# Where the next layer's conditioning sits in VectorE's queue during an MLP

## The chip, the cores and the metric

The kernel runs on one core of one Trainium2 chip. The metric is the device time of one execution in microseconds (us), as the median of several runs. The engines are named as in the profile: PE is TensorE's matmuls and PEld its weight loads, DVE is VectorE, ACT is ScalarE, POOL is GpSimd, and SP is SyncE, whose queue issues the loads that this text speaks of.

## The reference, cut to what matters

A transformer with 512 latent tokens, 256 context tokens and a width of 1024 runs two layers and then a second block with a mixture of experts. Every layer is conditioned on a vector: `silu(c) @ W + b` gives six vectors of 1024 (shift, scale and gate, for the mixer and for the MLP).

```python
def adaln(cond, w, b):
    return jnp.split(jax.nn.silu(cond) @ w + b, 6, axis=-1)

def squared_relu_mlp(h, w1, w2):
    return jnp.square(jax.nn.relu(h @ w1)) @ w2

# in each layer, after its mixer:
x = x + gt_m * squared_relu_mlp(modulate(x, sh_m, sc_m), mlp_w1[layer], mlp_w2[layer])
```

The MLP's hidden width is 4096. In layer 0 it also runs for the context tokens (768 tokens in all), in layer 1 for the 512 latent tokens alone. The conditioning of the latent tokens (`c`) needs all six vectors; that of the context (`c_ctx`) is computed for the first two.

## The kernel before

Activations lie transposed: eight tiles `x` of 128 features by 768 tokens. A product of full precision is made of three fast ones: weight and activation are each split into a high part (`wh`, `hh`) and a rest (`wl`, `hl`), and `dense` (L493) multiplies high by high, high by rest, rest by high. `load_w` brings a weight tile of 512 KB by SP's queue into one of three buffers, ACT makes `wh`, POOL makes `wl` (L471, L472, two buffers of each).

`mlp` works in four groups `g`. A group has eight **up tiles** (one weight tile each; PE fills a wide PSUM tile, of which there are two; ACT takes the ReLU into `u`, L615; DVE squares `u`, L616; ACT makes `hh`; DVE makes `hl`, L472) and then eight **down tiles** (one weight tile each; PE multiplies with the eight `hh` and `hl` of the group; DVE adds the result times the gate to `x`, L584, in `residual`). The first two up tiles are made together, as a pair. So each layer has 64 tiles: 32 up and 32 down. The first down tile of a group needs the `hh` and `hl` of the eighth up tile for the last eighth of its products.

Beside this, the MLP of one layer computes the conditioning of the next: `ada_side`. It needs 48 weight tiles `wside` of 128 x 1024 (512 KB each, two buffers, loaded by SP's queue, L457). A **pass** is one DVE instruction over such a tile (L460): multiply with the conditioning vector and sum along the row. The first two of the six vectors take two passes a tile, one for `c` and one for `c_ctx`; the others take one. That is 64 passes a layer. After the eighth tile of a vector a short instruction adds the bias (L462). The passes' list `side` is popped once per up tile and once per down tile, at the end of the tile's code:

```python
self.split(u[:, lo:hi], h[:, lo:hi], l[:, lo:hi])
hid.append((h, l))
if side:
    side.pop(0)()
```

The order of the code isn't the order in the engines' queues. The framework's scheduler orders each engine's instructions at build time, by which of them has its inputs ready in its own model of time; each engine then runs its queue strictly as written.

Of the kernel before, what the change touches and what calls it, by code (L numbers as in the profile page):

```python
# [10 lines left out]
F32 = mybir.dt.float32  # L11
# [4 lines left out]
ALU = mybir.AluOpType  # L16
# [6 lines left out]
D = 1024  # L23
# [282 lines left out]
class Kern:  # L306
# [135 lines left out]
    def ada_side(self, layer, pool):  # L442


        nc = self.nc
        cb = pool.tile([128, 2, D], F32, name="condb", bufs=1)
        nc.sync.dma_start(cb, self.i["cond"][layer - 1])
        nc.scalar.activation(cb, cb, AF.Silu)
        bias = self.p("ada_b_20" if layer == 2 else f"ada_b{layer}")

        def step(j, f):
            n = 2 if j < 2 else 1
            if f == 0:
                self.ada[layer, j] = self.const.tile([128, 8, 2], F32, name=f"ada{layer}_{j}")
            out = self.ada[layer, j]
            w = pool.tile([128, D], F32, tag="wside", name=self.uid("wside"), bufs=2)
            nc.sync.dma_start(w, self.i[f"ada{layer}"][8 * j + f])  # L457
            for q in range(n):
                o = pool.tile([128, D], F32, tag="side", name=self.uid("side"), bufs=1)
                nc.vector.scalar_tensor_tensor(o, w, 1.0, cb[:, q, :], op0=ALU.mult, op1=ALU.mult, accum_out=out[:, f, q:q + 1])  # L460
            if f == 7:
                nc.vector.scalar_tensor_tensor(out[:, :, :n], out[:, :, :n], 1.0 if j in (1, 4) else 0.0,  # L462
                                               bias[:, 8 * j:8 * j + 8, None].to_broadcast([128, 8, n]),
                                               op0=ALU.add, op1=ALU.add)

        return [lambda j=j, f=f: step(j, f) for j in (1, 0, 2, 4, 3, 5) for f in range(8)]


    def split(self, src, hi, lo, eng=None):
        nc = self.nc  # L470
        nc.scalar.activation(hi, src, AF.Copy)  # L471
        (eng or nc.vector).tensor_tensor(lo, src, hi.bitcast(F32), op=ALU.subtract)  # L472

    def load_w(self, src, n):

# [105 lines left out]

    def residual(self, x, ps, gt, f, parts):
        for q, (a, b) in enumerate(parts):
            self.nc.vector.scalar_tensor_tensor(x[:, a:b], ps[:, a:b], gt[:, f, q:q + 1], x[:, a:b],  # L584
                                                op0=ALU.mult, op1=ALU.add)


    def mlp(self, layer, parts):
        nc, tc = self.nc, self.tc
        lo, hi = parts[0][0], parts[-1][1]  # L590
        sh, sc, gt = (self.ada[layer, j] for j in (3, 4, 5))
        with tc.tile_pool(name=f"mlp{layer}", bufs=2, reuse_waits="tile") as pool:
            side = self.ada_side(layer + 1, pool)
            self.tb = 5

            def tmp(name):
                return pool.tile([128, TT], F32, tag="tmp", name=self.uid(name), bufs=self.tb)

            act = self.modulate(self.x, sh, sc, parts, pool)
            w1, w2 = self.i[f"mlp1_{layer}"], self.i[f"mlp2_{layer}"]  # L600

            first = self.dense_pair("up", [w1[0], w1[1]], act, parts)

            def up(g):
                hid = []
                for f in range(8 * g, 8 * g + 8):
                    if first:
                        ps = first.pop(0)
                    else:
                        ps = self.wide("up")  # L610
                        self.dense(ps, self.load_w(w1[f], 1024), act, parts)
                    u = pool.tile([128, TT], F32, tag="tmp", name=self.uid("u"), bufs=self.tb)
                    h = pool.tile([128, TT], F32R, tag="hh", name=self.uid("hh"), bufs=10)
                    l = pool.tile([128, TT], F32R, tag="hl", name=self.uid("hl"), bufs=10)
                    nc.scalar.activation(u[:, lo:hi], ps[:, lo:hi], AF.Relu)  # L615
                    nc.vector.tensor_tensor(u[:, lo:hi], u[:, lo:hi], u[:, lo:hi], op=ALU.mult)  # L616
                    self.split(u[:, lo:hi], h[:, lo:hi], l[:, lo:hi])
                    hid.append((h, l))
                    if side:
                        side.pop(0)()  # L620
                return hid

            if layer == 1:
                for k in range(KD):
                    nc.sync.dma_start(self.x[k][:, T:], self.i["ctx2T"][k])
            for g in range(4):
                hid = up(g)
                if g == 3:
                    acc = tmp("acc")
                for f in range(KD):  # L630
                    w = self.load_w(w2[g, f], 1024)
                    ps = self.wide("dn")
                    self.dense(ps, w, hid, parts)
                    self.residual(self.x[f], ps, gt, f, parts)
                    if g == 3:
                        self.squares_add(acc, self.x[f], f, PARTS, tmp, nc.gpsimd)
                    if side:
                        side.pop(0)()
            self.y = self.rstd_tokens(acc, PARTS)
            self.tb = 6  # L640

# [1815 lines left out]
```

## Time and profile before

| what | value |
|---|---|
| median of 3 runs | 3518.22 us (3511.94 to 3525.28) |
| the profiled execution's own time | 3523.28 us |
| span of that execution in the profile | 3521.4 us |
| MLP of layer 0 in the span | from about 588 to 1147 us |
| MLP of layer 1 in the span | from about 2221 to 2610 us |

The span runs from the first to the last instruction. A "wait" in the profile is the time that an engine stood idle before an instruction, with what ended it. An idle engine costs time only where something that sets the end waits for it.

### The profile page before, as it was taken

What the parts mean: (1) busy time and instruction counts of PE and PEld (TensorE: products, weight loads), DVE (VectorE), ACT (ScalarE), POOL (GpSimd) and SP (SyncE); (2) the same over time, 40 slices, a digit from 0 to 9 for tenths busy, and PEclk for the clock granted to TensorE, in tenths of its full rate; (3) what the DMA queues carried; (4) which work ended last, traced back from release to release, by engine and by line L of the source; (5) the groups of instructions that cost most, each with busy time, mean ns of one, the idle gap of its engine ahead of it and who ended that gap; (6) DMA issues with size and microseconds to landing.
All of it is one profiled execution on the core that took longest, in us unless ns stands there. A gap on an engine that the chain in (4) does not pass through costs nothing. (4 is left out here: it accounts for less than half of the span.)

```text
span 3521.4 us, 56690 instructions
## 1 busy us (share of the span) xinstructions
PE 3171.4 (90%) x23582; PEld 2413.3 (69%) x23582; DVE 1820.7 (52%) x3073; ACT 1320.0 (37%) x2503; POOL 913.9 (26%) x467
## 2 busy tenths in 40 slices
PE   7989998899999789589999998799999899799887
PEld 4666887788888677377887876677778677333333
DVE  5476664862322975477777763864342654222213
ACT  3232453211222543377777774322233453100001
POOL 1111113222324423422223212344443324100000
PEclk9999999999999899699999998999999999899999
DMA  5222222552222233200000103473332228799997
GB/s 220 96 72 84 84 73 96 186 185 66 64 63 98 85 106 109 69 18 28 28 28 28 31 8 114 161 251 126 94 115 67 75 78 274 274 420 421 420 421 312
DMA packets 126321, 488.44 MB, mean 139 GB/s; under 512 B 13360, under 2 KB 23024, under 8 KB 101744
## 3 DMA queue, kind: packets, MB, share of 16 engines
q1 hardware_dynamic: 119936, 477.40, 37.9%
q8 instruction: 186, 3.05, 0.4%
q0 software_dynamic: 1184, 4.20, 0.3%
q10 hardware_dynamic: 4944, 3.21, 0.3%
q14 instruction: 71, 0.58, 0.1%
HBM read 455.92 MB, written 28.84 MB: 138 GB/s over the span
## 5 line engine op out<-in xcount | busy, mean ns | idle before, releaser
L472 POOL TENSOR_TENSOR wl<-w,wh 128x1024 fp32r<-128x1024 f32 (+1 forms) x259 | 626.4, 2420 | 1602.2 <-ACT wh L471 1458.0
L471 ACT ACTIVATE wh<-w 128x1024 fp32r<-128x1024 f32 (+1 forms) x259 | 266.8, 1032 | 909.5 <-PE dn L493 333.6
L493 PE MATMUL dn<-hh,wh 128*128 128x512 f32 (+1 forms) x768 | 235.5, 361 | 18.3 <-ACT hh L471 16.5
L493 PE MATMUL up<-ah,wl 128*128 128x512 f32 (+1 forms) x768 | 235.9, 361 | 6.3 <-POOL wl L472 6.2
L493 PE MATMUL up<-ah,wh 128*128 128x512 f32 (+1 forms) x768 | 235.2, 361 | 5.9 <-ACT ah L576 2.8
L493 PE MATMUL dn<-hl,wh 128*128 128x512 f32 (+1 forms) x768 | 235.1, 360 | 2.3 <-DVE hl L472 2.3
L493 PE MATMUL dn<-hh,wl 128*128 128x512 f32 (+1 forms) x768 | 234.5, 359 | 2.3 <-POOL wl L472 2.2
L493 PE MATMUL up<-al,wh 128*128 128x512 f32 (+1 forms) x768 | 234.8, 360 | 0.9 <-DVE al L577 0.9
L460 DVE SCALAR_TENSOR_TENSOR side<-wside,condb 128x1024 f32<-128x1024 f32 x128 | 194.7, 1521 | 69.7 <-DMA wside<-ada 68.5
L616 DVE TENSOR_TENSOR u<-u 128x768 f32<-128x768 f32 (+1 forms) x64 | 126.9, 1986 | 128.8 <-ACT u L615 128.8
L584 DVE SCALAR_TENSOR_TENSOR x<-dn,ada,x 128x512 f32<-128x512 f32 x96 | 60.5, 657 | 255.6 <-PE dn L493 255.6
L493 PEld LDWEIGHTS dn<-hh,wh 128*128 128x128 f32 x768 | 128.5, 191 | 42.4 <-ACT hh L471 18.1
L493 PEld LDWEIGHTS up<-ah,wl 128*128 128x128 f32 x768 | 128.8, 191 | 31.6 <-POOL wl L472 10.0
L493 PEld LDWEIGHTS up<-ah,wh 128*128 128x128 f32 x768 | 129.2, 192 | 29.8 <-ACT ah L576 3.9
L493 PEld LDWEIGHTS dn<-hl,wh 128*128 128x128 f32 x768 | 128.6, 191 | 26.3 <-DVE hl L472 4.2
L493 PEld LDWEIGHTS dn<-hh,wl 128*128 128x128 f32 x768 | 128.5, 191 | 25.1 <-POOL wl L472 3.1
L493 PEld LDWEIGHTS up<-al,wh 128*128 128x128 f32 x768 | 128.8, 191 | 24.2 <-DVE al L577 2.0
L471 ACT ACTIVATE hh<-u 128x768 fp32r<-128x768 f32 (+1 forms) x64 | 47.3, 740 | 220.9 <-DVE u L616 220.9
L493 PE MATMUL p<-ah,wh 128*128 128x512 f32 (+1 forms) x320 | 116.9, 394 | 2.2 <-ACT ah L576 1.2
L493 PE MATMUL rp<-xl,wh 128*128 128x512 f32 x368 | 109.2, 361 | 10.5 <-DVE xl L472 10.4
L493 PE MATMUL rp<-xh,wh 128*128 128x512 f32 x368 | 109.6, 364 | 9.1 <-ACT xh L471 7.9
L493 PE MATMUL p<-ah,wl 128*128 128x512 f32 x320 | 112.7, 381 | 2.1 <-POOL wl L472 2.1
(623 smaller groups left out, 7427.9 us busy)
## 6 DMA issues: line engine op xcount, KB each, us to landing
w<-mlp SPq DMA_DIRECT2D x128, 512.0 KB, 3.7
wside<-ada SPq DMA_DIRECT2D x96, 512.0 KB, 4.1
ew<-e_gate SPq DMA_DIRECT2D x45, 1024.0 KB, 19.8
ew<-e_up SPq DMA_DIRECT2D x41, 1024.0 KB, 21.1
ew<-e_down SPq DMA_DIRECT2D x39, 1024.0 KB, 19.8
wada<-ada SPq DMA_DIRECT2D x48, 512.0 KB, 3.6
ewm<-e_up SPq DMA_DIRECT2D x18, 1024.0 KB, 20.0
ewm<-e_down SPq DMA_DIRECT2D x18, 1024.0 KB, 19.8
```

What stands on the lines that cost most here:

```text
L460: nc.vector.scalar_tensor_tensor(o, w, 1.0, cb[:, q, :], op0=ALU.mult, op1=ALU.mult, accum_out=out[:, f, q:q + 1])
L471: nc.scalar.activation(hi, src, AF.Copy)
L472: (eng or nc.vector).tensor_tensor(lo, src, hi.bitcast(F32), op=ALU.subtract)
L493: nc.tensor.matmul(ps[:, a:b], ww[:, 128 * k:128 * k + 128], aa[:, a:b], start=(first and k == 0 and q == 0), stop=(last and k == nk - 1 a ...
L584: self.nc.vector.scalar_tensor_tensor(x[:, a:b], ps[:, a:b], gt[:, f, q:q + 1], x[:, a:b], op0=ALU.mult, op1=ALU.add)
L616: nc.vector.tensor_tensor(u[:, lo:hi], u[:, lo:hi], u[:, lo:hi], op=ALU.mult)
```

## The change

One list entry is now one pass, not one weight tile with its one or two passes: the list has 64 entries instead of 48. After an up tile one entry is taken; after a down tile two in the first two groups and one later. Each entry is traced within `issue_after`, which records for the DVE instructions in it that they come behind a given DVE instruction in the queue: behind the `hl` of that up tile, or behind the last `x` of that down tile. The load of `wside`, on SP's queue, gets no such edge. To give the instruction back, `split` and `residual` return what they issued last.

```diff
-        def step(j, f):
-            n = 2 if j < 2 else 1
-            if f == 0:
+        def step(j, f, q, n, st={}):
+            if f == q == 0:
                 self.ada[layer, j] = self.const.tile([128, 8, 2], F32, name=f"ada{layer}_{j}")
             out = self.ada[layer, j]
-            w = pool.tile([128, D], F32, tag="wside", name=self.uid("wside"), bufs=2)
-            nc.sync.dma_start(w, self.i[f"ada{layer}"][8 * j + f])
-            for q in range(n):
-                o = pool.tile([128, D], F32, tag="side", name=self.uid("side"), bufs=1)
-                nc.vector.scalar_tensor_tensor(o, w, 1.0, cb[:, q, :], op0=ALU.mult, op1=ALU.mult, accum_out=out[:, f, q:q + 1])
-            if f == 7:
+            if q == 0:
+                st["w"] = pool.tile([128, D], F32, tag="wside", name=self.uid("wside"), bufs=2)
+                nc.sync.dma_start(st["w"], self.i[f"ada{layer}"][8 * j + f])
+            o = pool.tile([128, D], F32, tag="side", name=self.uid("side"), bufs=1)
+            nc.vector.scalar_tensor_tensor(o, st["w"], 1.0, cb[:, q, :], op0=ALU.mult, op1=ALU.mult, accum_out=out[:, f, q:q + 1])
+            if f == 7 and q == n - 1:
...
-        return [lambda j=j, f=f: step(j, f) for j in (1, 0, 2, 4, 3, 5) for f in range(8)]
+        parts = {j: 2 if j < 2 else 1 for j in range(6)}
+        return [partial(step, j, f, q, parts[j]) for j in (1, 0, 2, 4, 3, 5) for f in range(8) for q in range(parts[j])]
...
+            def beside(ins, n=1):
+
+                with tc.issue_after(ins.ins):
+                    for _ in range(min(n, len(side))):
+                        side.pop(0)()
...
-                    self.split(u[:, lo:hi], h[:, lo:hi], l[:, lo:hi])
+                    beside(self.split(u[:, lo:hi], h[:, lo:hi], l[:, lo:hi]))
                     hid.append((h, l))
-                    if side:
-                        side.pop(0)()
...
-                    self.residual(self.x[f], ps, gt, f, parts)
+                    ins = self.residual(self.x[f], ps, gt, f, parts)
                     if g == 3:
                         self.squares_add(acc, self.x[f], f, PARTS, tmp, nc.gpsimd)
-                    if side:
-                        side.pop(0)()
+                    beside(ins, 2 if g < 2 else 1)
```

## Rows read from the trace of the kernel before

**Rows 1.** The page: busy time of an engine, share of the span, instructions.
```profile
PE 3171.4 (90%) x23582; PEld 2413.3 (69%) x23582; DVE 1820.7 (52%) x3073; ACT 1320.0 (37%) x2503; POOL 913.9 (26%) x467
```

**Rows 2.** Windows, layer 0: us; busy (instructions) PE, PEld, DVE, ACT, POOL; clock; DMA share; GB/s.
```profile
664.00:684.00 20.00, 10.59 (x44) 8.56 (x44) 16.14 (x20) 4.40 (x5) 5.00 (x2) 0.68 0.63 215
...
847.00:900.00 53.00, 53.00 (x308) 46.98 (x308) 10.83 (x13) 8.81 (x10) 16.87 (x7) 1.00 0.19 60
```

**Rows 3.** Windows, layer 1, same columns.
```profile
2264.00:2289.00 25.00, 18.08 (x70) 13.29 (x70) 24.50 (x34) 7.86 (x11) 9.20 (x3) 0.93 0.58 189
...
2436.00:2500.00 64.00, 63.77 (x274) 50.92 (x273) 28.63 (x20) 20.16 (x27) 28.30 (x12) 1.00 0.30 91
```

**Rows 4.** Waits, 600 to 780 us: us in total, times, longest.
```profile
ACT hh L471 <- DVE u L616: 57.2, 11, 8.9
DVE side L460 <- DMA wside<-ada: 35.3, 27, 3.5
...
PE dn L493 <- ACT hh L471: 8.5, 1, 8.5
```

**Rows 5.** Timeline of DVE in layer 0's first group: start, us, instruction.
```profile
656.51 3.46 DVE L460 SCALAR_TENSOR_TENSOR side<-wside,condb 128x1024 f32<-128x1024 f32 x1
...
663.70 0.95 DVE L616 TENSOR_TENSOR u<-u 128x768 f32<-128x768 f32 x1
```

**Rows 6.** Timeline of PE in layer 0: the idle stretches up to 800 us.
```profile
607.29 0.61 PE L493 MATMUL up<-ah,wh 128*128 128x512 f32 x2 [0.46 <-ACT u L615]
...
610.13 1.01 PE L493 MATMUL up<-ah,wl 128*128 128x512 f32 x2 [1.86 <-POOL wl L472]
...
676.73 1.01 PE L493 MATMUL dn<-hh,wh 128*128 128x512 f32 x2 [8.46 <-ACT hh L471]
```

**Rows 7.** Timeline of PE in layer 1: behind the first pair, and a later up-to-down border.
```profile
2235.76 0.50 PE L493 MATMUL up<-ah,wh 128*128 128x512 f32 x1 [0.75 <-ACT u L615]
...
2237.71 0.67 PE L493 MATMUL up<-ah,wl 128*128 128x512 f32 x1 [1.22 <-POOL wl L472]
...
2479.24 0.51 PE L493 MATMUL dn<-hl,wh 128*128 128x512 f32 x1 [0.23 <-DVE hl L472]
```

**Rows 8.** Timeline of DVE in layer 0: down tiles, second of group 1, last of group 3.
```profile
829.81 1.14 DVE L584 SCALAR_TENSOR_TENSOR x<-dn,ada,x 128x512 f32<-128x512 f32 x2 [7.18 <-PE dn L493]
...
1145.96 1.14 DVE L584 SCALAR_TENSOR_TENSOR x<-dn,ada,x 128x512 f32<-128x512 f32 x2 [7.17 <-PE dn L493]
```

**Rows 9.** Timeline of DVE in layer 1: down tiles, last of group 1, last of group 3.
```profile
2429.09 0.75 DVE L584 SCALAR_TENSOR_TENSOR x<-dn,ada,x 128x512 f32<-128x512 f32 x1 [4.85 <-PE dn L493]
...
2609.33 0.75 DVE L584 SCALAR_TENSOR_TENSOR x<-dn,ada,x 128x512 f32<-128x512 f32 x1 [4.86 <-PE dn L493]
```

**Rows 10.** Timeline of DVE in layer 0: a late up tile, no passes left.
```profile
1055.94 2.57 DVE L616 TENSOR_TENSOR u<-u 128x768 f32<-128x768 f32 x1 [3.88 <-ACT u L615]
1059.42 0.96 DVE L472 TENSOR_TENSOR hl<-u,hh 128x768 fp32r<-128x768 f32 x1 [0.91 <-ACT hh L471]
```

**Rows 11.** Timeline of DVE in layer 1: a late up tile, no passes left.
```profile
2441.68 2.51 DVE L616 TENSOR_TENSOR u<-u 128x512 f32<-128x512 f32 x1 [1.70 <-ACT u L615]
2444.89 0.69 DVE L472 TENSOR_TENSOR hl<-u,hh 128x512 fp32r<-128x512 f32 x1 [0.70 <-ACT hh L471]
```

**Rows 12.** Timeline of POOL in layer 1, beside the up tile of rows 11.
```profile
2441.24 2.40 POOL L472 TENSOR_TENSOR wl<-w,wh 128x1024 fp32r<-128x1024 f32 x1 [3.20 <-ACT wh L471]
2446.84 2.40 POOL L472 TENSOR_TENSOR wl<-w,wh 128x1024 fp32r<-128x1024 f32 x1 [3.20 <-ACT wh L471]
```

**Rows 13.** Tile `side`, both layers: count, ns least/median/most, first and last start.
```profile
L460 DVE SCALAR_TENSOR_TENSOR side<-wside,condb x128: 1207/1225/3460, 602.6 to 2397.5; 128x1024 f32<-128x1024 f32 x128
```

**Rows 14.** DMA issues, 2210 to 2430 us: count, KB each, median us to landing.
```profile
wside<-ada SPq DMA_DIRECT2D x48, 512.0 KB, 4.3
```

**Rows 15.** Timeline of DVE in layer 1, group 1's up tiles: first and sixth of six.
```profile
2353.87 1.22 DVE L460 SCALAR_TENSOR_TENSOR side<-wside,condb 128x1024 f32<-128x1024 f32 x1 [2.47 <-DMA wside<-ada]
...
2383.94 1.22 DVE L460 SCALAR_TENSOR_TENSOR side<-wside,condb 128x1024 f32<-128x1024 f32 x1 [2.35 <-DMA wside<-ada]
```

More of the change, by code (lines that the diff above doesn't have):

```diff
@@ L471, in split @@
         nc.scalar.activation(hi, src, AF.Copy)
-        (eng or nc.vector).tensor_tensor(lo, src, hi.bitcast(F32), op=ALU.subtract)
+        return (eng or nc.vector).tensor_tensor(lo, src, hi.bitcast(F32), op=ALU.subtract)
     def load_w(self, src, n):
@@ L583, in residual @@
         for q, (a, b) in enumerate(parts):
-            self.nc.vector.scalar_tensor_tensor(x[:, a:b], ps[:, a:b], gt[:, f, q:q + 1], x[:, a:b],
-                                                op0=ALU.mult, op1=ALU.add)
+            ins = self.nc.vector.scalar_tensor_tensor(x[:, a:b], ps[:, a:b], gt[:, f, q:q + 1], x[:, a:b],
+                                                      op0=ALU.mult, op1=ALU.add)
+        return ins
     def mlp(self, layer, parts):
```

## The prediction

> **What bounds the kernel now.** I read the page first: PE is busy 90% of the span [rows 1], so time can be won only where PE stands still or runs at a lower clock. The passes run in both MLPs, the first at 602.6 and the last at 2397.5 us [rows 13], so I read the windows of both. Where no passes are left, layer 0 executes 308 matmuls in 53 us with PE busy throughout and the clock at 1.00 [rows 2]; where they run, the window from 664 to 684 us has 44 matmuls in 20 us, PE busy 10.59 us, DVE busy 16.14 us, clock 0.68. At 308/53 = 5.81 matmuls a us, 20 us should hold 116, so (116 - 44)/5.81 = 12.4 us are lost in this window alone. Layer 1 has the same picture: 70 matmuls in 25 us with DVE busy 24.50, against 274 in 64 us later [rows 3].
>
> Then the waits say who is late. Between 600 and 780 us ACT waited 57.2 us for DVE's square `u` before it could make `hh`, and PE 8.5 us for `hh` [rows 4]; in the timeline this is the 8.46 us at 676.73, the border from up tiles to down tiles, and the two matmuls that end it take 1.01 us as the clock comes back [rows 6]. DVE is late because several passes stand in its queue between one `hl` and the next `u`: from the pass at 656.51 to `u` at 663.70 there are 7.2 us, filled by four passes, one of 3.46 us [rows 5]. On top of that DVE waits for the passes' own loads, 35.3 us in 27 waits [rows 4].
>
> Last I measured the whole loss by tile counts. In layer 0's clean part a tile takes 7.18 + 1.14 = 8.32 us, and 38 tiles from 829.81 to 1145.96 take 316.15 = 38 x 8.32: nothing lost there [rows 8]. The first pair ended at 607.29 - 0.46 = 606.83 [rows 6]; 24 tiles later, at 829.81, 222.98 us have gone instead of 24 x 8.32 = 199.7. **Layer 0 loses 23.3 us.** In layer 1 a clean tile takes 4.85 + 0.75 = 5.60 us [rows 9]; the pair ended at 2235.76 - 0.75 = 2235.01 [rows 7]; 30 tiles later, at 2429.09, 194.1 us have gone instead of 168.0: **layer 1 loses 26.1 us.** The 32 tiles after that take 180.24 instead of 179.2.
>
> **The change, part by part.** The number of passes (64 a layer), loads (48) and bias instructions stays; nothing is removed but the backlog. *Layer 0, up tile.* A clean up tile on DVE is 3.88 idle + 2.57 `u` + 0.91 idle + 0.96 `hl` [rows 10]. A pass takes 1.22 us at the median [rows 13]; with the reading of its sum I count 1.33 (the four passes of [rows 5] take 7.19, and 7.19 - 3.46 leaves 1.24 for each of the others, so 1.33 is on the safe side). It fits in the 3.88: cost nothing. *Layer 0, down tile.* `x` 1.14 plus two passes at worst 3.46 + 1.33 is 5.93 of 8.32 [rows 8, 13]: nothing. *Layer 1, up tile.* DVE idles 1.70 us between `hl` and the next `u` [rows 11]; a pass of 1.33 leaves 0.37. POOL's `wl` would be the trouble: `u` takes 2.51 us there since it overlaps `wl`. But `hl` ends at 2444.89 + 0.69 = 2445.58, the pass would end at 2446.9, and the next `wl` starts at 2446.84 [rows 12]: it fits, narrowly. Cost nothing; without that cover, a pass late by one `wl` (2.40) would hold the next `u` back by about 2 us.
>
> *Layer 1, down tile, groups 0 and 1.* `x` 0.75 + two passes 2.66 + one `wl` in the way 2.40 = 5.81 against 5.60: 0.21 late a tile, 16 tiles, so between 0 (`x` need only be done before PE wants that PSUM tile again, a tile later, and DVE idles 4.85 of each clean tile [rows 9]) and 3.4 us. In group 1 each pass also needs its own load. Two loads and a weight load per tile is the traffic that up tiles of group 1 have now: five tiles from 2353.87 to 2383.94, 6.01 us each [rows 15], with 4.3 us from issue to landing [rows 14]. That is 0.41 over 5.60 for eight down tiles, 0 to 3.3 us. For both together I take 2.5 of at most 6.7, nearer the low end since one tile of PSUM slack swallows the first 4.85 us. *Borders.* The up-to-down border of layer 1 has no slack even clean: PE waited 0.23 us for `hl` [rows 7]. A pass that slips ahead of the eighth `u` costs at most 1.33, three borders: 0 to 4 us; I take 1.0.
>
> *What stays.* Behind the pair, PE waits 0.46 + 1.86 us in layer 0 and 0.75 + 1.22 in layer 1 for the ReLU and for `wl` [rows 6, 7]; these come from the two buffers of split weights and the two PSUM tiles, which the pair fills, not from passes. The lower clock behind them costs about 1.5 more each (an estimate: the two matmuls at 610.13 take 1.01 us where 2/5.81 = 0.34 is the clean pace [rows 2, 6], and since neighbours overlap I count half of the 0.67 between them, for four or five such steps). So 3.8 us of layer 0's and 3.5 of layer 1's loss stay; the bounds are none of it and all 7.3.
>
> *Queues.* Behind a waiting pass stand the next `u`, `hl` or `x`, and behind those ACT's `hh`, `wh` and PE. The loads of `wside` stand in SP's queue among the weight loads: a `wside` waiting for its buffer, now freed by passes that come later, holds up the weight loads behind it. Weights lie three tiles ahead, so a delay under a tile costs nothing; a delay of `wside` itself reaches DVE only in the layer 1 case above. The conditioning is done at the end of group 2 instead of early in group 1; two groups' borders and eight down tiles still follow before the next stage reads it: nothing.
>
> A rule that could speak against the placing: the Trainium skill, SBUF — State Buffer, section "Who interferes with whom", has VectorE instructions with two SBUF inputs and GpSimd instructions that read SBUF exclude each other for a whole instruction, and issue order decides who waits. The trace agrees: 1.207 against 3.460 us for the same pass [rows 13]. By the rule alone DVE loses at most one `wl` a tile however the passes lie, which is the 0.21 above and no more.
>
> **Sum.** Layer 0: 23.3 - 3.8 = 19.5. Layer 1: 26.1 - 3.5 - 2.5 - 1.0 = 19.1. Together 38.6 us: the profiled execution's own 3523.28 (span 3521.4 plus 1.9 around it) becomes 3484.7. It lies 5.1 above the median of the runs, 3518.22; against that median I forecast 3480.
>
> **Rivals.** (a) *Layer 1 keeps the pace of its loads*: every tile with a pass there still takes 6.01. 46 tiles after the pair, 46 x 0.41 = 18.9 lost again; layer 1 gains 26.1 - 3.5 - 18.9 = 3.7, together 23.2: 3495. For it: the 0.37 us of room and 4.3 us landing; against it: only eight tiles need two loads. (b) *The wait takes the place of the backlog*: slower. Each pass, now fixed in front of the next `u`, finds its load late, as the 27 waits of at most 3.5 us do now [rows 4]; DVE can't go around it. Layer 1's up tile becomes 2.51 + 0.70 + 0.69 + 1.33 + 3.5 = 8.73, 24 of them at 3.1 over; layer 0's 2.57 + 0.91 + 0.96 + 1.33 + 3.5 = 9.27, 24 at 0.95: 98 us against the 42.1 won: 3574. It decides from a wait of 2.1 us in every up tile on: 24 x (2.1 - 0.37) = 42. For it: weight loads ahead of `wside` in SP's queue that wait for their own buffer. Against: a load is asked for two passes ahead, a tile or more against 4.3 us. The Trainium skill, TensorE: Matmul & The Clock Gate, first table, calls VectorE's queue strictly first-in first-out, which is this rival's ground; the trace agrees so far that `u` stood behind four passes [rows 5]. (c) *Nothing changes*: the queue's order stays as it was, or the stall reappears at later borders (six borders of 7 us would eat the gain; the worst now is 8.46): 3518.
>
> **Chances.** Forecast 0.68, (a) 0.14, (c) 0.08, (b) 0.10. The range: at best both losses vanish whole, 49.4 us, and the run lies low in its spread (6 us): 3462. At the top it takes in (a) with its room: 3504, leaving (b) and (c) out. The likeliest case alone is 3466 to 3490. Half a per cent is 17.6 us, about what a measurement here can tell from nothing; faster takes the forecast and most of (a): 0.80, same 0.10, slower 0.10.
>
> **What would show it.** In the profile after: one pass behind each `hl`, one or two behind each `x`, until the end of group 2; `hh` no longer waiting long for `u`; no 8 us idle of PE near 670; clock 1.00 in those windows; up tiles every 8.32 and 5.60 us. DVE's waits for `wside` should nearly vanish but for layer 1's group 1. The prediction is wrong if `u` or `x` waits behind a pass that waits for its load in most tiles, or if weight loads land late behind `wside`.

## The result, and the profile after

The changed kernel takes 3478.48 us (median of 4 runs, 3474.83 to 3481.87) against 3517.19 of the kernel before (the median of four runs; the 3518.22 above is that of three of them): a ratio of 0.9888, 95% interval 0.9872 to 0.9903. It is faster by 39 us, clear of the scatter, and the forecast was 3480.

The page of the changed kernel answers to [rows 1]; every engine executes as many instructions as before, but DVE is busy for 66 us longer. More of its instructions run beside POOL's `wl`: a pass takes 1.77 us on average where it took 1.52, a square 2.53 where it took 1.99.

```profile
span 3476.8 us, 56676 instructions
...
PE 3154.3 (91%) x23582; PEld 2405.0 (69%) x23582; DVE 1886.9 (54%) x3073; ACT 1321.2 (38%) x2503; POOL 915.7 (26%) x467
```

The windows of the changed kernel, with the columns of [rows 2]; the third lies in layer 1's first group and answers to [rows 3]:

```profile
664.00:684.00 20.00, 20.00 (x117) 17.72 (x116) 13.26 (x16) 2.56 (x3) 4.82 (x2) 1.00 0.49 148
847.00:900.00 53.00, 53.00 (x308) 46.98 (x308) 30.55 (x31) 12.65 (x15) 14.45 (x6) 1.00 0.49 157
2244.00:2269.00 25.00, 24.78 (x107) 19.59 (x106) 21.89 (x24) 7.27 (x9) 12.63 (x5) 1.00 0.51 165
```

From 664 to 684 us PE now executes 117 matmuls at clock 1.00, where it had 44 at 0.68; the 308 in the later 53 us haven't changed. In the 25 us of layer 1 it executes 107 where it had 70. DVE is nearly as busy in layer 1's first group as before (21.89 of 25 us, against 24.50), yet PE stands still for 0.2 us: what counts isn't how much DVE does but in which order.

The waits from 600 to 780 us, to be held against [rows 4]:

```profile
DVE u L623 <- ACT u L622: 36.6, 13, 4.2
ACT hh L471 <- DVE u L623: 34.9, 14, 2.6
```

ACT's wait for the square lasts 2.6 us at the longest, the length of the square itself (2.57 in the lines below); it was 8.9. Now DVE waits for ACT's ReLU. No wait of DVE for a load and none of PE for `hh` is left in this stretch.

The timeline of DVE in layer 0, an up tile and a down tile of the first group, at the same times as [rows 5]:

```profile
652.08 2.57 DVE L623 TENSOR_TENSOR u<-u 128x768 f32<-128x768 f32 x1 [2.73 <-ACT u L622]
655.56 0.96 DVE L472 TENSOR_TENSOR hl<-u,hh 128x768 fp32r<-128x768 f32 x1 [0.91 <-ACT hh L471]
656.43 1.22 DVE L459 SCALAR_TENSOR_TENSOR side<-wside,condb 128x1024 f32<-128x1024 f32 x1
...
675.54 1.14 DVE L584 SCALAR_TENSOR_TENSOR x<-dn,ada,x 128x512 f32<-128x512 f32 x2 [2.71 <-PE dn L493]
676.60 3.27 DVE L459 SCALAR_TENSOR_TENSOR side<-wside,condb 128x1024 f32<-128x1024 f32 x1
...
679.91 1.23 DVE L459 SCALAR_TENSOR_TENSOR side<-wside,condb 128x1024 f32<-128x1024 f32 x1
```

One pass stands behind `hl`, two behind `x`, and each tile has 2.7 us to spare: the up tile the 3.88 of [rows 10] less one pass of 1.22, the down tile the 7.18 of [rows 8] less passes of 3.27 and 1.23.

The idle stretches of PE in the two MLPs up to the first border of layer 1, beside [rows 6, 7]:

```profile
607.57 0.62 PE L493 MATMUL up<-ah,wh 128*128 128x512 f32 x2 [0.46 <-ACT u L622]
609.36 0.62 PE L493 MATMUL up<-ah,wl 128*128 128x512 f32 x2 [0.83 <-POOL wl L472]
...
2214.12 0.50 PE L493 MATMUL up<-ah,wh 128*128 128x512 f32 x1 [0.75 <-ACT u L622]
2216.07 0.51 PE L493 MATMUL up<-ah,wl 128*128 128x512 f32 x1 [1.22 <-POOL wl L472]
2254.86 0.50 PE L493 MATMUL dn<-hl,wh 128*128 128x512 f32 x1 [0.22 <-DVE hl L472]
```

The 8.46 us at the border are gone. Behind the pairs the waits are those of before, but for `wl` in layer 0: 0.83 instead of 1.86.

From its first matmul to the start of its last addition to `x`, layer 0's MLP takes 536.90 us instead of 558.36, layer 1's 365.10 instead of 388.77: 21.46 and 23.67, together 45.1 us. These lengths are the measure in all that follows. The spans differ by 44.6 us.

### The profile page after: what moved, and what is told of

Same layout as the page of the kernel before. It is cut to its first block, busy times and chain, and to the rows that moved or that the text cites. A ratio compares the mean times of both kernels' runs of the same rounds, so it can differ in the third digit from the quotient of the medians.

```text
span 3476.8 us, 56676 instructions
## 1 busy us (share of the span) xinstructions
PE 3154.3 (91%) x23582; PEld 2405.0 (69%) x23582; DVE 1886.9 (54%) x3073; ACT 1321.2 (38%) x2503; POOL 915.7 (26%) x467
## 3 DMA queue, kind: packets, MB, share of 16 engines
q1 hardware_dynamic: 119936, 477.40, 38.6%
## 5 line engine op out<-in xcount | busy, mean ns | idle before, releaser
L459 DVE SCALAR_TENSOR_TENSOR side<-wside,condb 128x1024 f32<-128x1024 f32 x128 | 226.2, 1768 | 17.3 <-DMA wside<-ada 16.2
L623 DVE TENSOR_TENSOR u<-u 128x768 f32<-128x768 f32 (+1 forms) x64 | 161.9, 2532 | 128.8 <-ACT u L622 128.7
L2400 ACT ACTIVATE xT<-ed,tcol 128x512 fp32r<-128x512 f32 (+1 forms) x17 | 11.2, 661 | 273.4 <-issue 184.8
```

Of the source, the lines that this page charges most:

```text
L459: nc.vector.scalar_tensor_tensor(o, st["w"], 1.0, cb[:, q, :], op0=ALU.mult, op1=ALU.mult, accum_out=out[:, f, q:q + 1])
L2400: nc.scalar.activation(yh[:, s], pd[hf][:, cut], AF.Copy, scale=tcol[:, 0, p:p + 1])
```

## The experiments

### The change again, in more rounds

> The changed kernel as it is, in more rounds, since the two profiled executions lie 44.6 us apart and the medians 38.7. Theory: the two MLPs give back 45 us in every execution, and the rest of the span scatters by some 7 us from one execution to the next, so the ratio comes out between 0.987 and 0.989 (39 to 46 us), with MLPs of 537 and 365 us. Rival (the MLPs themselves scatter): their lengths differ from the first profile of the change by more than 2 us.

Measured: 3479.74 us, ratio 0.9886 (0.9867 to 0.9906), MLPs of 536.90 and 365.14 us. The changed kernel's MLPs repeat to 0.04 us; its scatter lies elsewhere. In the thirteen profiled executions of this study the stretch between the two MLPs takes from 1068.0 to 1075.9 us, and both profiles of the change are at 1075.2 (the one of before is at 1074.6). So the 45 us in the profiles and the 38 to 39 in the medians are compatible, and the interval reaches from 33 to 47 us. What makes that stretch scatter stays open.

### Grain without order

```diff
-                with tc.issue_after(ins.ins):
-                    for _ in range(min(n, len(side))):
-                        side.pop(0)()
+                for _ in range(min(n, len(side))):
+                    side.pop(0)()
```

> Grain without order: single passes, one or two a tile as in the change, but without the edge to the tile's last DVE operation. Theory: the passes stand in VectorE's queue where they stood before, several ahead of each square, so the time is that of the kernel before, 3517, with PE idle some 8 us at the first up-to-down border. Rival (the finer list itself spreads the passes): 3478 to 3500.

Measured: 3519.83 us, ratio 1.001 (0.9999 to 1.0022), MLPs of 556.34 and 388.80 us. In the traces of both MLPs DVE executes passes, squares and additions in exactly the order of before. Layer 0's MLP is 2.0 us shorter than in the profile of before all the same, so an MLP with that order is known to some 2 us only, and the 45.1 us with it. PE's idle stretch at the border is back:

```profile
678.60 1.01 PE L493 MATMUL dn<-hh,wh 128*128 128x512 f32 x2 [8.62 <-ACT hh L471]
```

The finer list alone is worth nothing: the scheduler moves the passes forward, whatever tile they were traced beside. That it does so because its model of time sees DVE free there is the reading that fits; how far it moves them changes with the loads, as the later kernels show.

### Order without grain

```diff
-        def step(j, f, q, n, st={}):
+        def step(j, f):       # both passes of a weight tile, as before
...
-                    beside(ins, 2 if g < 2 else 1)
+                    beside(ins)
```

> Order without grain: a list entry is again a whole weight tile with its one or two passes, one entry per tile as before, but traced behind the tile's last DVE operation. Theory (the loss was the backlog that the queue's order made): nearly all is won. In layer 1's first group an up tile on DVE takes 2.51 + 0.70 + 0.69 + 2 x 1.33 = 6.56 us against 5.60, 0.96 over for some six tiles, so about 5 us stay lost there: 3483. Layer 0 has room (7.1 of 8.32). Rival (single passes matter as much as the order): about half is won, 3498.

Measured: 3485.84 us, ratio 0.9916 (0.99 to 0.9933), MLPs of 536.98 and 373.65 us. The order gives all of layer 0 and 15.1 of 23.7 us of layer 1; the finer grain, with fewer passes in an up tile of the first group, gives the last 8.5, more than the 5 expected. DVE in layer 1's first group, an up tile, and PE's wait at the border that follows:

```profile
2222.25 1.22 DVE L460 SCALAR_TENSOR_TENSOR side<-wside,condb 128x1024 f32<-128x1024 f32 x1
...
2223.51 3.30 DVE L460 SCALAR_TENSOR_TENSOR side<-wside,condb 128x1024 f32<-128x1024 f32 x1
...
2226.73 0.68 DVE L623 TENSOR_TENSOR u<-u 128x512 f32<-128x512 f32 x1
2228.11 0.69 DVE L472 TENSOR_TENSOR hl<-u,hh 128x512 fp32r<-128x512 f32 x1 [0.70 <-ACT hh L471]
```

```profile
2253.96 0.50 PE L493 MATMUL dn<-hh,wh 128*128 128x512 f32 x1 [4.09 <-ACT hh L471]
2254.68 0.79 PE L493 MATMUL dn<-hl,wh 128*128 128x512 f32 x1 [0.23 <-DVE hl L472]
```

Squares follow each other every 6.47 us (2226.73, 2233.20) where PE needs 5.60. Six tiles make 5.2 us of lateness; PE waits 4.09 for it at the border and 0.60 for `wl` before three of the tiles. Behind the border it runs for a while at a lower clock (0.72 granted from 2253 to 2259 us), which takes part of the rest.

### The edge in layer 0 alone

```diff
-                with tc.issue_after(ins.ins):
+                with tc.issue_after(ins.ins) if layer == 0 else ExitStack():
```

> The change with its edge in layer 0's MLP alone; in layer 1 the passes stand as before. Theory (each layer's loss is its own): layer 0's MLP takes 537 us from its first matmul to its last addition to x, as in the profile of the change, layer 1's 389 as before, and the time is 3517.8 - 21 = 3497. Rival (the gain comes from one layer, or through what the MLP leaves to the next stage): 3517 or 3478.

Measured: 3501.28 us, ratio 0.9955 (0.9939 to 0.9972), MLPs of 536.91 and 389.12 us. Each layer's gain is its own: the lengths are those of the change in layer 0 and of before in layer 1, and the ratio's interval, 10 to 21 us, just reaches the 21 expected. The stretch between the MLPs is 1068.0 us here, behind an MLP as long as in the change, so the order in the MLP alone doesn't set it.

### What the passes in front of a square cost: their time or their loads

Three kernels without the edge, in which each pass is short, or has no load to wait for, or both. The scheduler orders them itself, and not as before: it moves more of them forward. Ahead of a square of layer 0's first group stood three or four passes before; now there are up to six short ones, or up to five with few loads (and six between the additions of two down tiles); with both cuts all 64 passes of a layer stand ahead of its fourth square. The three kernels show what passes cost where the scheduler puts them, not the two costs at one fixed order.

```diff
 # short: 8 of 1024 columns
-nc.vector.scalar_tensor_tensor(o, w, 1.0, cb[:, q, :], op0=ALU.mult, op1=ALU.mult, accum_out=out[:, f, q:q + 1])
+nc.vector.scalar_tensor_tensor(o[:, :8], w[:, :8], 1.0, cb[:, q, :8], op0=ALU.mult, op1=ALU.mult, accum_out=out[:, f, q:q + 1])
 # few loads: one per vector
-            w = pool.tile([128, D], F32, tag="wside", name=self.uid("wside"), bufs=2)
-            nc.sync.dma_start(w, self.i[f"ada{layer}"][8 * j + f])
+            if f == 0:
+                st["w"] = pool.tile([128, D], F32, tag="wside", name=self.uid("wside"), bufs=2)
+                nc.sync.dma_start(st["w"], self.i[f"ada{layer}"][8 * j + f])
+            w = st["w"]
```

> The kernel before with every pass cut to 8 of its 1024 columns, all 48 loads a layer kept; the conditioning of the next layer is thus summed over 8 inputs only. Theory (DVE's time in the passes makes the backlog): a pass falls from 1.2 to about 0.1 us, the squares come in time though several passes stand ahead of each, and 30 to 40 us are won: about 3480. Rival (DVE waits for the passes' loads, and those make it late): the waits stay and grow, 3505 or more.

> The kernel before with one load of conditioning weights per vector instead of eight (6 a layer instead of 48), all 64 passes kept at full length; seven of eight passes use the wrong weight tile. Theory (pass time): DVE's waits for loads vanish, but the backlog of passes ahead of the squares is as long, so at least two thirds of the loss stay: 3500 to 3520. Rival (loads): the loss goes with the waits, about 3480.

> The kernel before with both cuts together: passes over 8 of 1024 columns and one load per vector instead of eight (the conditioning of the next layer is summed over 8 inputs of the wrong tiles). The queue's order is left as the scheduler makes it. Theory (the order costs only through what the passes ahead of a square take or wait for, and either alone is enough): with neither, the whole loss is gone, 3472 to 3478. Rival (the order itself costs, or the loss lies elsewhere in the MLP): 3490 or more.

| kernel, without the edge | time, us | ratio (interval) | MLP 0 | MLP 1 |
|---|---|---|---|---|
| short passes, all loads | 3499.63 | 0.9951 (0.9934 to 0.9967) | 548.16 | 375.03 |
| full passes, few loads | 3525.22 | 1.0015 (1.0005 to 1.0025) | 557.19 | 393.89 |
| short passes, few loads | 3479.03 | 0.9886 (0.9869 to 0.9902) | 537.26 | 367.53 |

The waits from 600 to 790 us, first with short passes, then with few loads:

```profile
DVE side L460 <- DMA wside<-ada: 72.3, 42, 3.6
...
ACT hh L471 <- DVE u L616: 47.8, 13, 7.3
```

```profile
ACT hh L473 <- DVE u L618: 56.3, 12, 8.9
...
PEld dn L495 <- ACT hh L473: 9.6, 2, 8.3
```

My expectation for the short passes was wrong: I counted the time in the passes as the cause and expected 3480. With the passes cut, to 0.17 us at the median, DVE reaches the next one sooner and waits for its load instead. The waits double against [rows 4] (72.3 us against 35.3, and all of them lie before 780 us too), ACT still waits up to 7.3 us for a square, and only about half of the loss goes. Past the two idle stretches that follow each pair, PE waits in both layers for `hh`, `hl` and `x` alone (4.16 us the longest), never for a weight tile, so it isn't weight loads held up by the other loads that cost here. Without the loads the passes alone hold the squares back as long as ever (8.9), and none of the loss goes; layer 1 is even 5 us longer, with PE waiting for `x` six times behind the longer rows of passes. With both gone the MLPs are within 2.8 us of the change's. So passes and loads are two covers of one fault: what stands ahead of the square in DVE's queue makes it late by its time or by its wait, and either alone was enough to keep half of the loss or all of it.

### One buffer: the price of late loads

```diff
-tag="wside", name=self.uid("wside"), bufs=2)
+tag="wside", name=self.uid("wside"), bufs=1)
```

> The change with one buffer for the conditioning's weight tiles instead of two, so that a load can start only when the pass before it is done and each pass finds its load late. It puts a price on rival (b). Theory (a pass that waits holds up what stands behind it): where two loads are needed in a tile (down tiles of group 1), a tile takes 2 x (1.33 + 4.7) = 12.1 us, 3.8 over in layer 0 and 6.5 in layer 1, 8 tiles each: 82; where two passes share a load in one tile (down tiles of group 0) 2.66 + 4.7 = 7.4, over in layer 1 alone: 14; with the tile that the PSUM buffers absorb taken off, about 80 slower than the change: 3560. Rival (waits for loads stay hidden): 3478.

Measured: 3490.27 us, ratio 0.9928 (0.9911 to 0.9944), MLPs of 538.49 and 379.61 us: 16 us more than the change in the MLPs, and 11 to 12 in the medians, not 80. DVE's waits over both layers, its timeline in a stretch of layer 1's group 1 where two passes a tile were traced, and an up tile of layer 1's group 2:

```profile
  DMA wside<-ada: 170.4, 66
```

```profile
2351.68 0.75 DVE L584 SCALAR_TENSOR_TENSOR x<-dn,ada,x 128x512 f32<-128x512 f32 x1 [0.53 <-PE dn L493]
2355.56 1.23 DVE L459 SCALAR_TENSOR_TENSOR side<-wside,condb 128x1024 f32<-128x1024 f32 x1 [3.14 <-DMA wside<-ada]
...
2357.28 0.75 DVE L584 SCALAR_TENSOR_TENSOR x<-dn,ada,x 128x512 f32<-128x512 f32 x1 [0.48 <-PE dn L493]
...
2412.17 1.22 DVE L459 SCALAR_TENSOR_TENSOR side<-wside,condb 128x1024 f32<-128x1024 f32 x1 [2.57 <-DMA wside<-ada]
2413.32 0.69 DVE L623 TENSOR_TENSOR u<-u 128x512 f32<-128x512 f32 x1
```

Several things were wrong in my price. A load lands 3.7 us after its issue at the median, where I had counted 4.7. The edge says "not before", not "here": with the loads late in its model too, the scheduler put one pass behind each `x` and moved the rest to later tiles, so that the last one starts at 2531.1 us instead of 2475.7. And a wait of some 3 us behind `x` is free as long as the next `x` comes within PE's spare PSUM tile. Even in front of a square one such wait a tile is cheap here: in the up tiles of layer 1's group 2 every pass waits 2.0 to 4.2 us for its load, most of it while `wl` runs, and the square behind it takes 0.69 us instead of the 2.51 that it takes beside `wl`. Squares come every 5.9 us instead of 5.60, and PE pays at the borders of groups 2 and 3, with waits for `hh` of 3.97 and 3.90 us. The waits are ten times those of the change (16.2 us in 10), and cost a tenth of their sum.

### Every pass twice: the room in each kind of tile

```diff
+            for _ in range(2):
-            nc.vector.scalar_tensor_tensor(o, st["w"], 1.0, cb[:, q, :], op0=ALU.mult, op1=ALU.mult, accum_out=out[:, f, q:q + 1])
+                nc.vector.scalar_tensor_tensor(o, st["w"], 1.0, cb[:, q, :], op0=ALU.mult, op1=ALU.mult, accum_out=out[:, f, q:q + 1])
```

> The change with every pass issued twice in a row (the second repeats the first's work). It tests the room that the prediction counted in each kind of tile. Layer 0 up: 2.57 + 0.91 + 0.96 + 2.66 = 7.1 of 8.32, nothing. Layer 0 down with two entries: 1.14 + 5.32 + 2.40 = 8.86, 0.54 x 16 = 9. Layer 1 up: 2.51 + 0.70 + 0.69 + 2.66 = 6.56 of 5.60, 0.96 x 24 = 23. Layer 1 down with two entries: 0.75 + 5.32 + 2.40 = 8.47, 2.87 x 16 = 46. Together 78, less some 10 that the spare PSUM tile takes up: 3546. Rival (DVE has far more room than counted, since the profile calls it 54% busy): 3478 to 3490.

Measured: 3529.09 us, ratio 1.0026 (1.0016 to 1.0035), MLPs of 536.93 and 415.27 us. Layer 0 takes twice the passes at no cost at all; I had counted 9 us over in its down tiles, and they just fit:

```profile
692.17 1.14 DVE L585 SCALAR_TENSOR_TENSOR x<-dn,ada,x 128x512 f32<-128x512 f32 x2 [0.18 <-PE dn L494]
693.23 3.27 DVE L460 SCALAR_TENSOR_TENSOR side<-wside,condb 128x1024 f32<-128x1024 f32 x1
```

Layer 1 loses 50.2 us where 59 were expected (69 less 10): `x` followed `x` from 2264.32 to 2295.59 in four tiles of 7.8 us, where I had counted 8.47. The idea that DVE, busy 54% of the span, has room everywhere is refuted: the room is in layer 0's tiles.

### One pass behind each of the 64 tiles

```diff
-                    beside(ins, 2 if g < 2 else 1)
+                    beside(ins)
```

> The change with one pass behind every tile of all four groups, never two. The prediction took 2.5 us for the down tiles of layer 1 with two passes and up to 6.7. Theory (the spare PSUM tile takes all of it up): the time is that of the change, 3478, layer 1's MLP 365 us, though DVE's waits for the passes' loads (16 us in the change) go to nothing. Rival (the prediction's 2.5): 3475, layer 1's MLP 362 to 363.

Measured: 3479.85 us, ratio 0.9887 (0.9869 to 0.9905), MLPs of 537.23 and 365.13 us. DVE no longer waits for a load of `wside` at all, and nothing is won: the tiles with two passes cost the change nothing.

### The pass behind the square

```diff
-                    nc.vector.tensor_tensor(u[:, lo:hi], u[:, lo:hi], u[:, lo:hi], op=ALU.mult)
-                    beside(self.split(u[:, lo:hi], h[:, lo:hi], l[:, lo:hi]))
+                    beside(nc.vector.tensor_tensor(u[:, lo:hi], u[:, lo:hi], u[:, lo:hi], op=ALU.mult))
+                    self.split(u[:, lo:hi], h[:, lo:hi], l[:, lo:hi])
```

> The change with the pass of an up tile traced behind its square instead of behind its hl, so that it stands between the two, where DVE waits for ACT anyway (0.91 us in layer 0, 0.70 in layer 1). Theory (layer 1's up-to-down border has no slack): a pass of 1.33 makes hl 0.63 later in layer 1 and PE's wait at the borders goes from 0.22 to about 0.85 us, three borders: layer 1's MLP 367, layer 0's 537, the time 3480, not to be told from the change. Rival (the place behind the last operation is what wins): each up tile loses 0.63, layer 1's MLP 380 or more, 3493.

Measured: 3474.21 us, ratio 0.9873 (0.9855 to 0.989), MLPs of 537.32 and 366.19 us; its interval shares more than half of its width with the change's (0.9867 to 0.9906 beside it), so the lower median says nothing. DVE in an up tile of layer 1, and PE at the border:

```profile
2405.92 2.51 DVE L623 TENSOR_TENSOR u<-u 128x512 f32<-128x512 f32 x1 [0.93 <-ACT u L622]
2408.36 1.21 DVE L459 SCALAR_TENSOR_TENSOR side<-wside,condb 128x1024 f32<-128x1024 f32 x1
...
2409.50 0.68 DVE L472 TENSOR_TENSOR hl<-u,hh 128x512 fp32r<-128x512 f32 x1
```

```profile
2438.23 0.50 PE L493 MATMUL dn<-hl,wh 128*128 128x512 f32 x1 [0.58 <-DVE hl L472]
```

The border costs 0.58 instead of 0.22, three times: 1.1 us, which is what layer 1's MLP is longer. It isn't the place behind the very last operation that wins, but that no more passes stand between two squares than the up tile has room for: one in layer 1, two in layer 0, where the kernel with every pass twice lost nothing.

## Why the prediction was right

**The loss and its place.** The 23.3 and 26.1 us by tile counts were the right sums to work from. The same count in the profile after: layer 0's pair ends at 607.57 - 0.46 = 607.11 and the addition 24 tiles later starts at 808.66, 201.55 us instead of 199.68, so 1.9 us are lost of 23.3. In layer 1, from 2214.12 - 0.75 = 2213.37 to 2441.44, 40 tiles take 228.07 instead of 224.0: 4.1 us lost, 0.7 of it at three borders. Over all 62 tiles behind the pair layer 1 lost 27.1 us before and loses 4.6 now.

**The cause.** A backlog of passes and their waits in front of each square: shown by the grain alone (no gain), the order alone (most of it), and the three kernels without the edge. The prediction named both covers, 7.2 us of passes [rows 5] and 35.3 us of waits [rows 4], but not that either alone keeps half of the loss up, or all of it.

**The sizes.** 19.5 us were forecast for layer 0, and 21.5 came; 19.1 for layer 1, and 23.7 came. Three terms were off. *What stays* in layer 0, 3.8 us, measured 1.9: PE's wait for `wl` behind the pair fell to 0.83, and the matmul behind it is at full pace (0.62 us for two where [rows 6] has 1.01). From 609 to 614 us the granted clock is 1.00, with 27 matmuls, where it was 0.66, with 14. So part of what I called structural belonged to the passes. *The down tiles of layer 1*, 2.5 us, measured 0: one pass a tile gives the same 365.13 us. DVE was late there, and did wait 16.2 us for loads:

```profile
2357.29 0.75 DVE L584 SCALAR_TENSOR_TENSOR x<-dn,ada,x 128x512 f32<-128x512 f32 x1
2361.00 1.23 DVE L459 SCALAR_TENSOR_TENSOR side<-wside,condb 128x1024 f32<-128x1024 f32 x1 [2.97 <-DMA wside<-ada]
...
2363.42 0.75 DVE L584 SCALAR_TENSOR_TENSOR x<-dn,ada,x 128x512 f32<-128x512 f32 x1
```

But here, in the changed kernel's group 1, PE had no idle stretch: `x` 6.13 us apart, and 8.10 us the next time, stayed within the spare PSUM tile. *The borders*, 1.0 us for a pass that slips, measured 0: each costs 0.22, as a border without passes did (0.23 in [rows 7]). Besides, the pair of layer 1 took 13.3 us instead of 14.5, since no pass stands among its `al` any more; I hadn't counted that. One reading was loose: that the passes were done "early in group 1" before holds for layer 0 alone; in layer 1 the last one, at 2397.5 us [rows 13], stood among group 1's down tiles. It changes no term.

**The total.** The MLPs gave 45.1 us, 6.5 more than the 38.6 forecast; the medians gave 38.7 and 38.2. That the forecast of 3480 met the measured time to 1.5 us is luck: the profiled execution of before lies 5 to 6 us above its median, those of the change at theirs, and the stretch outside the MLPs scatters by more than these differences. Whether it is also a little longer in the change stays open.

**The rivals.** (a) fell: tiles of layer 1 with a pass keep 5.60 us. (c) fell, though the kernel with the grain alone is just that case. (b) was the right kind of danger at the wrong price: I priced it as if every pass were nailed to its tile and every wait reached PE, and I counted a square's 2.51 us beside `wl` on top of a wait in which `wl` had run; with one buffer 170 us of waits cost 16. Its ground held: with short passes DVE executed a square whose ReLU had ended at 644.2 us only at 649.88, behind waits of 1.00 and 3.16 us for loads that the square doesn't need. The Trainium skill, TensorE: Matmul & The Clock Gate, first table, calls VectorE's queue strictly first-in first-out; the trace agrees.

## What to carry to other kernels

Filler work that a scheduler may place freely can end up in front of the work that feeds the bound engine, as it did here with up to four passes ahead of a square. Tie each piece behind an instruction of the tile that has room for it, and take the room from one clean tile of each kind: idle time between its instructions on that engine, not the engine's share of the span. Making only the filler shorter, or only its loads fewer, didn't cure the order: half of the loss stayed, or all of it.

## What the runs showed of the hardware that I had not expected

Moving the passes also sped up a POOL instruction that the change doesn't touch: PE's wait for the third `wl` of layer 0 fell from 1.86 to 0.83 us when no pass ran beside it. A pass at 606.63 us stood just ahead of it, and POOL's two `wl` from 606.68 on took 6.44 us; in the change, from 606.95 on, they take 5.44. The Trainium skill, SBUF — State Buffer, section "Who interferes with whom", lets a VectorE instruction with two SBUF inputs hold up a GpSimd instruction as well as the other way round; the trace agrees. My sum had only counted POOL in DVE's way. In layer 0's first group, where a down tile's first pass meets `wl` every time, it takes 3.27 us instead of 1.22, and this costs nothing.
